# Four narrow full-precision products side by side, and more rooms for what feeds them, in a one-core hybrid decoder step

## The chip, the core and the metric

One core of one Trainium2 chip runs the whole step as one program. The metric is the time of one execution in device microseconds; the kernel before has a median of 2964.94 us over three runs (2961.44 to 2966.86). The engines are named as the profile names them: PE (matrix products), PEld (its weight loads), DVE (vector), ACT (scalar), POOL, and SP, which here only issues DMAs. Each engine runs its own instructions in order.

## What is computed

One layer of a decoder for two groups of tokens that share the weights: a prompt of 2048 tokens, and 32 sample tokens (8 requests of 4 tokens) with states and caches of their own. Cut to what matters:

```python
m, s_gla, s_ssm, conv = mixer(rmsnorm(x, g1), s_gla, s_ssm, conv, lw)   # GLA heads beside Mamba-2 heads; ends in @ w_out
h = x + rmsnorm(m, g2)
q = rmsnorm(h, g3) @ w_xq                                # 4 heads of 256
p = softmax(q @ mem_k.T / 16);  a = (p @ mem_v) @ w_xo   # 256 memory tokens
h = h + rmsnorm(a, g4)
hf = rmsnorm(h, g5)
y = h + rmsnorm((silu(hf @ w_gate) * (hf @ w_up)) @ w_down, g6)         # 2816 features
```

All of it is float32. The outputs are `y` of both groups, the new states, the convolution tails, and the memory keys and values of the prompt.

## The kernel before

**The prompt** comes first in blocks of 512 tokens (function `block`: projections, convolution, both kinds of heads), then in passes of Strassen-like products: `o` (w_out), `s` and `v` (cross-attention, with the weights folded), three passes `g` (gate and up), and four passes `d` (w_down, 2 or 3 of the 11 feature pairs each, 8 units of 256 tokens per pass). A product of two float32 numbers is made of three `fp32r` products (`three`, L125 to L127), for which ACT and DVE split each operand into a larger and a smaller part (L1540/L1542 for the tokens, in tiles `s`; L1609/L1613 for the weights, in tiles `r`). A unit is seven such products in the order `TURN`; each is called an element here. Their sums sit in PSUM banks `accA`, `accB`, `accC`, and ACT (L1920 in the `d` passes) or DVE take them out.

**The weights of a pass** come in pieces (`Pieces`): a piece is loaded into one of three rooms `st` (SP, L1645), split into a room `r`, and the room `st` is loaded again. A pass `d` of three feature pairs has 14 pieces, a pass of two has 7. The pieces of the next pass are made known at the start of the last unit but one (three loads go out), and one piece is split after each element of the last unit; the rest follow in the first unit of the new pass. There are 8 rooms `r`, and a room is taken again only when its old content is used up.

**The 32 sample tokens** have no stage of their own. Their work stands in generators (`samples`, `sample_chunk`, `samples_down`), and each `yield` ends a step. After each element the main loop takes 0.4 steps (in `g`, from the queue `back`) or 0.8 steps (in `d`, from `aux`). Their products are true float32 with only 32 columns of the PE array: the output goes to one of four groups of 32 columns (`tile_position=(0, 32 * g)`), and PE makes two passes over the moving data for each.

- `s_proj` (L1229; w_out, w_xq and w_xo): a step loads 512 KB into one of two rooms `sraw`, and multiplies with two column groups.
- `s_attend` (L1307): scores against the cached keys; a step of four products takes two products in one column group and two in another. The values (L1342): a step of four products, one in each group.
- `samples_down` (L1958): 44 products; a step is one product, with five rooms `w` of 256 KB.
- `sample_mixer`: 8 states of each kind are read twice, each load (`gla_state`, `ssm_state`; L980, L985) going out in the step that uses it, into two rooms.

**In the last pass `d`** each half unit of results lives in one of seven rooms `y`: taken out of PSUM, `yp` (the earlier passes' sum) added by a DMA, normed, `hX` added by a DMA, stored (L1883). For the last two units `yp` and `hX` are read into spare rooms from the start of the last unit but two (L2122, L2123), one of them a room `y`.

**Order.** In the passes the main loop's instructions are pinned to program order on each engine (`pin`); those of the queue `back` in `g`, and the blocks before, are placed by the framework's scheduler. `quad_sums` (L413 to L422) works in block 1 on sums of w_out: two loads, two empty steps, four subtractions on DVE, four stores.

Of the kernel before, what the change touches and what calls it, by code (L numbers as in the profile page):

```python
# [42 lines left out]
def hymba_kernel(ctx: ExitStack, tc: tile.TileContext, a: dict, o: dict, dbg: dict | None = None):  # L43
# [34 lines left out]
    def drain(q):  # L78
        while q:
            step(q)  # L80


    NJ = seq // 256
# [322 lines left out]
    def quad_sums(i, w):  # L406
        pa2 = late["pa2"]
        for u in range(4):
            for c in (slice(0, 256), slice(256, 512)):
                t = []  # L410
                for n in range(2):
                    r = pa2.tile([P, 512], F32, name="fold", bufs=2)
                    nc.gpsimd.dma_start(out=r.rearrange("p (k c) -> p k c", k=2), in_=w[n, u].rearrange("p (k c) -> p k c", k=2)[:, :, c])  # L413
                    t += [r[:, 0:256], r[:, 256:512]]
                r = pa2.tile([P, 2, MEM], F32, name="fraw")
                t += [r[:, 0], r[:, 1]]
                yield
                yield
                for out, x, y in ((4, 2, 0), (5, 3, 4), (2, 3, 2), (1, 1, 5)):
                    nc.vector.tensor_tensor(t[out], t[x], t[y], op=ALU.subtract)  # L420
                for q, at in enumerate((4, 5, 2, 1)):
                    nc.gpsimd.dma_start(out=wX[i, q][:, u, c], in_=t[at])  # L422
                yield
# [506 lines left out]
    def sample_mixer():  # L930
      mixS, rsel, rmk = (sm2[n] for n in ("mixS", "rsel", "rmk"))
      with ExitStack() as mctx:
# [42 lines left out]
        nc.vector.memset(par[64:128, 1:2], 1.0)  # L975


        def gla_state(r):
            t = mt_([P, 2, P], "Gs", bufs=2)
            nc.sync.dma_start(out=t, in_=a["state_gla"][r])  # L980
            return t

        def ssm_state(r):
            t = mt_([P, 512], "Ms", bufs=2)
            nc.sync.dma_start(out=t, in_=a["state_ssm"][r])  # L985
            return t


        yield
# [228 lines left out]


    def s_proj(units, act, out, ss, gain):  # L1220
        for n in range(2):
            ps = mxt()
            for u in range(4):
                w = ps_.tile([P, 1024], F32, name="sraw", bufs=2)
                nc.sync.dma_start(out=w, in_=units[n, u])
                for kk in range(2):
                    kt = 2 * u + kk
                    g0 = (kt % 4) * 32
                    nc.tensor.matmul(ps[g0:g0 + 32], lhsT=act[:, kt], rhs=w[:, kk * 512:(kk + 1) * 512], start=kt < 4, stop=kt >= 4,  # L1229
                                     tile_position=(0, g0))  # L1230
                yield
            sl = slice(n * 512, (n + 1) * 512)
            fold(out[:, sl], ps)
            if ss is not None:
                nc.scalar.activation(ps[:NS], out[:, sl], AF.Square, accum_out=ss[:NS, n:n + 1])
                ga = post_gain(ps_, "ga", gain, n)
                nc.vector.tensor_tensor(out[:, sl], out[:, sl], ga[:NS], op=ALU.mult)

    def s_T(src, gain, scale):
# [46 lines left out]
    def s_attend():  # L1286
# [4 lines left out]

        def load(i):
            if i < 2 * NR:
                t = ps_.tile([P, 4, MEM], F32, name="sraw", bufs=2)
                nc.sync.dma_start(out=t, in_=a["cache_k"][i // 2][:, i % 2 * 4:i % 2 * 4 + 4])
                got.append(t)
        load(0)
        load(1)
        yield
        for r in range(NR):  # L1300
            qm = ps_.tile([P, KT, NS], F32, name="sqm", bufs=1)
            nc.vector.tensor_tensor(qm, q, sm2["rmk"][:, r].rearrange("p s t -> p (s t)").unsqueeze(1).broadcast_to([P, KT, NS]), op=ALU.mult)
            for kt in range(KT):
                hd = kt // 2
                if kt % 4 == 0:
                    kr = got.popleft()
                nc.tensor.matmul(psc[32 * hd:32 * hd + 32, 0:MEM], lhsT=qm[:, kt], rhs=kr[:, kt % 4], start=r == 0 and kt % 2 == 0,  # L1307
                                 stop=r == NR - 1 and kt % 2 == 1, tile_position=(0, 32 * hd))
                if kt % 4 == 3:
                    load(2 * r + kt // 4 + 2)  # L1310
                    yield
        nm = small.tile([P, 8], F32, name="nm")
        sm = small.tile([P, 8], F32, name="sm")
        nc.vector.tensor_reduce(nm[:, 0:1], psc[:, 0:MEM], axis=mybir.AxisListType.X, op=ALU.max, negate=True)
# [12 lines left out]

        def load(i):
            if i < 2 * NR:
                t = ps_.tile([P, D], F32, name="sraw", bufs=2)  # L1330
                nc.sync.dma_start(out=t, in_=a["cache_v"][i // 2][:, i % 2])
                got.append(t)
        load(0)
        load(1)
        yield
        for r in range(NR):
            pm_ = ps_.tile([P, 8, NS], F32, name="sqm", bufs=1)
            nc.vector.tensor_tensor(pm_, pT, sm2["rmk"][:, r].rearrange("p s t -> p (s t)").unsqueeze(1).broadcast_to([P, 8, NS]), op=ALU.mult)
            for mt in range(2):
                vr = got.popleft()  # L1340
                for hd in range(4):
                    nc.tensor.matmul(po[32 * hd:32 * hd + 32, 0:256], lhsT=pm_[:, 4 * mt + hd], rhs=vr[:, hd * 256:(hd + 1) * 256],  # L1342
                                     start=r == 0 and mt == 0, stop=r == NR - 1 and mt == 1, tile_position=(0, 32 * hd))
                load(2 * r + mt + 2)
                yield
        ot = ps_.tile([P, MEM], F32, name="sp_", bufs=1)
        nc.vector.tensor_copy(ot, po[:, 0:256])
# [537 lines left out]
    def after_direct(j, m, y, ss, h, last):  # L1885

        if not last:
            yield
        if last:
            nc.scalar.activation(mxt(), half(y)[0], AF.Square, accum_out=ss[:, 0:1])  # L1890
            nc.vector.tensor_tensor(half(y)[1], half(y)[1], half(gain["ln_ffn_post"])[1], op=ALU.mult)
            rs = rstd_rows(ss)
            nc.vector.tensor_tensor(half(y)[0], half(y)[0], half(gain["ln_ffn_post"])[0], op=ALU.mult)
            for n in (1, 0):
                t = half(y)[n]
                nc.vector.scalar_tensor_tensor(t, t, rs[:, 0:1], half(h)[n], op0=ALU.mult, op1=ALU.add)
# [40 lines left out]
    def samples_down():  # L1937

        m = pd.tile([P, D], F32, name="m")[:NS]
        ss = small.tile([P, 8], F32, name="s_sq", bufs=1)  # L1940
        ws = deque()

        def load(i):
            if i < 2 * FT:
                n, kt = divmod(i, FT)
                w = pd.tile([P, 512], F32, name="w", bufs=5)
                nc.sync.dma_start(out=w, in_=a["w_down"][n, kt // 2, :, (kt % 2) * 512:(kt % 2 + 1) * 512])
                ws.append(w)
        for i in range(4):
            load(i)  # L1950
        yield
        yield
        for n in range(2):
            ps = mxt()
            for kt in range(FT):
                load(n * FT + kt + 4)
                g0 = (kt % 4) * 32
                nc.tensor.matmul(ps[g0:g0 + 32], lhsT=s_f[:, kt].rearrange("p h t -> p (h t)"), rhs=ws.popleft(),  # L1958
                                 start=kt < 4, stop=kt >= FT - 4, tile_position=(0, g0))
# [46 lines left out]
    def enter(k):  # L2006
# [20 lines left out]
        if kind == "d" and i == 0:  # L2027
# [4 lines left out]
            pd.tile([P, 512], F32, name="w", bufs=5)  # L2032
            gain_row(pd, "ln_ffn_post")
            aux.append(samples_down())
            ring[:] = 8, pd
# [60 lines left out]
    for e, (n, i) in enumerate(order):  # L2096
        k, g, left = work[n]
        kind, b, gs = passes[k]
        if i == 0:
# [11 lines left out]
            elif kind == "d":  # L2111
                if n + 3 == len(work):
# [1 line left out]
                    k8 = made[0] % 8  # L2114
                    r = f((ring[1] if k8 == 7 else rp).tile([P, 2 * RW], F32R, name=f"r{k8}"))
                    rooms = [r[:, c * D:(c + 1) * D] for c in range(3)] + [pd.tile([P, D], F32, name="m")]
                    rooms += [stage() for _ in range(3)] + [pd.tile([P, D], F32, name="y", bufs=7)]
                    adds = []
                    for j in (g + 1, g + 2):
                        z, h = [rooms.pop(0), rooms.pop(0)], [rooms.pop(0), rooms.pop(0)]  # L2120
                        for m in range(2):
                            nc.sync.dma_start(out=z[m], in_=yp[j][:, m * D:(m + 1) * D])  # L2122
                            nc.sync.dma_start(out=h[m], in_=hX[rows(j, m)])  # L2123
# [31 lines left out]
            fn()  # L2155
        part(e + ahead_)

        p = coming if work[cur][2] == 1 else now if begins[cur] else None
        if p:
            p.larger()  # L2160
        tick()
# [114 lines left out]
```

## Time and profile before

| What | us or share |
|---|---|
| median of 3 runs | 2964.94 |
| the profiled execution: its time | 2965.97 |
| its span, first to last instruction | 2964.2 |
| PE busy | 2830.4 (95%) |
| DVE busy | 2089.2 (70%) |
| ACT busy | 1526.3 (51%) |
| mean DMA rate | 179 GB/s |
| mean granted PE clock | 0.983 |

How to read the rows that follow in the prediction. A row of the timeline has the start, the length, the engine, the line, what it writes and reads, and how many instructions are merged (`x8`); a bracket tells how long the engine was idle before and what ended that. A row of windows has a stretch of time, its length, the busy time of PE, PEld, DVE, ACT and POOL (with counts of instructions), the granted PE clock, the busy share of the DMA engines, and GB/s. A row of groups has the line, the operation, its tiles, the count, the busy time and the mean length in ns of one. A row of waits has who waited for whom: us in total, times, the longest. A full matmul's row is longer than its share of time, since matmuls are pipelined: time is read from start to start.

### The profile page before, as it was taken

Reading aid. Unit: us, or ns where it says so; the run is one execution under the profiler, and the core shown is the slowest. Engines: PE = TensorE matmul, PEld = TensorE weight load, DVE = VectorE, ACT = ScalarE, POOL = GpSimd, SP = SyncE. Lnnn points to the kernel's source line nnn. Section 1 sums busy time; section 2 is a strip of 40 time slices with the busy share of each in tenths; the row PEclk is TensorE's granted clock in tenths of the full one; section 3 lists DMA queues with packets and bytes.
Section 4 is the critical chain, followed back from the end, with each engine's and each line's share of the span. In section 5 each row is a group of like instructions: output and inputs, shape, how many; then the busy total and the mean of one; then the engine's idle time right before and its main releaser. Section 6 shows DMA issues by size and latency. Waiting matters only on the chain.

```text
span 2964.2 us, 42292 instructions
## 1 busy us (share of the span) xinstructions
PE 2830.4 (95%) x15207; PEld 2385.0 (80%) x15207; DVE 2089.2 (70%) x3915; ACT 1526.3 (51%) x3047; POOL 554.2 (19%) x754
## 2 busy tenths in 40 slices
PE   8999899999988999999899999999999999999996
PEld 8887677787866878888798977889999985587774
DVE  7677676666737787777887867667678884556565
ACT  5545443544446786767655334434455553434453
POOL 2142341221321321035302100001000000011122
PEclk9999999999999999999999999999999999999998
DMA  7345544242256875568745567663243345767797
GB/s 243 121 147 174 174 123 130 80 126 88 79 201 231 295 266 202 189 193 259 257 158 196 173 199 259 221 222 138 95 153 121 126 165 188 234 144 180 169 224 212
DMA packets 154849, 530.02 MB, mean 179 GB/s; under 512 B 19392, under 2 KB 22640, under 8 KB 143120
## 3 DMA queue, kind: packets, MB, share of 16 engines
q1 hardware_dynamic: 93216, 331.81, 34.8%
q0 software_dynamic: 49184, 170.52, 18.7%
q10 hardware_dynamic: 12240, 24.99, 2.6%
q8 instruction: 120, 1.97, 0.3%
q14 instruction: 89, 0.73, 0.1%
HBM read 373.10 MB, written 154.15 MB: 178 GB/s over the span
## 4 chain that ended last, share of the span: by engine, by line
PE 49%; issue 25%; DVE 7%; DMA 5%; ACT 4%; POOL 2%; POOLq 0%; DVEq 0%; ACTq 0%; SPq 0%
PE accA L125 6%; PE accA L126 6%; PE accA L127 6%; PE acc L125 4%; PE acc L126 4%; PE acc L127 4%; PE accC L125 3%; PE accC L127 3%; PE accC L126 3%; PE accB L125 1%; PE mx L1958 1%; PE accB L127 1%; PE accB L126 1%; DVE s L1542 1%; ACT r L1609 1%
## 5 line engine op out<-in xcount | busy, mean ns | idle before, releaser
L125 PE MATMUL accA<-r,s 128*128 128x512 f32 (+2 forms) x1792 | 643.6, 359 | 27.3 <-ACT r L1609 6.8
L127 PE MATMUL accA<-r,s 128*128 128x512 f32 (+2 forms) x1792 | 631.6, 352 | 2.0 <-DVE s L1542 1.9
L126 PE MATMUL accA<-r,s 128*128 128x384 f32 (+2 forms) x1600 | 556.6, 348 | 1.8 <-DVE r L1613 1.8
L125 PEld LDWEIGHTS accA<-r,s 128*128 128x128 f32 x1792 | 340.8, 190 | 103.4 <-issue 24.2
L1540 ACT ACTIVATE s<-sum 128x512 fp32r<-128x512 f32 (+2 forms) x488 | 289.0, 593 | 249.4 <-DVE sum L1522 103.2
L127 PEld LDWEIGHTS accA<-r,s 128*128 128x128 f32 x1792 | 341.0, 190 | 35.2 <-DVE s L1542 3.6
L125 PE MATMUL accC<-r,s 128*128 128x512 f32 (+2 forms) x896 | 322.7, 360 | 27.2 <-ACT y L1920 15.9
L1542 DVE TENSOR_TENSOR s<-sum,s 128x512 fp32r<-128x512 f32 (+2 forms) x488 | 310.6, 644 | 29.6 <-ACT s L1540 23.6
L126 PEld LDWEIGHTS accA<-r,s 128*128 128x128 f32 x1600 | 304.7, 190 | 25.4 <-DVE r L1613 3.9
L127 PE MATMUL accC<-r,s 128*128 128x512 f32 (+2 forms) x896 | 315.8, 352 | 0.2 <-DVE s L1542 0.2
L1542 DVE TENSOR_TENSOR s<-raw,s 128x512 fp32r<-128x512 f32 (+2 forms) x366 | 236.0, 645 | 70.5 <-ACT s L1540 69.2
L126 PE MATMUL accC<-r,s 128*128 128x384 f32 (+2 forms) x800 | 277.9, 347 | 0.3 <-DVE r L1613 0.3
L1540 ACT ACTIVATE s<-raw 128x512 fp32r<-128x512 f32 (+2 forms) x366 | 218.2, 596 | 64.8 <-PE accC L127 59.2
L119 ACT ACTIVATE whi<-wraw 128x1024 fp32r<-128x1024 f32 (+2 forms) x148 | 137.1, 941 | 196.3 <-PE acc L126 99.4
L125 PEld LDWEIGHTS accC<-r,s 128*128 128x128 f32 x896 | 170.4, 190 | 67.7 <-ACT y L1920 22.2
L120 DVE TENSOR_TENSOR wlo<-wraw,whi 128x1024 fp32r<-128x1024 f32 (+2 forms) x148 | 165.1, 1125 | 58.6 <-ACT whi L119 55.8
L127 PEld LDWEIGHTS accC<-r,s 128*128 128x128 f32 x896 | 170.2, 190 | 16.9 <-DVE s L1542 0.9
L125 PE MATMUL acc<-xh,whi 128*128 128x512 f32 (+1 forms) x464 | 168.7, 365 | 8.4 <-ACT xh L280 8.2
L133 POOL TENSOR_TENSOR rs<-ms,nhalf 128x1 f32<-128x1 f32 (+4 forms) x125 | 113.9, 913 | 329.2 <-DVE ms L131 312.9
L127 PE MATMUL acc<-xh,wlo 128*128 128x512 f32 (+1 forms) x464 | 164.9, 357 | 1.7 <-DVE wlo L120 1.7
L126 PE MATMUL acc<-xl,whi 128*128 128x512 f32 (+1 forms) x464 | 164.4, 356 | 0.2 <-DVE xl L281 0.2
L126 PEld LDWEIGHTS accC<-r,s 128*128 128x128 f32 x800 | 152.7, 191 | 10.7 <-DVE r L1613 0.6
(650 smaller groups left out, 5922.2 us busy)
## 6 DMA issues: line engine op xcount, KB each, us to landing
raw<-in_w_gu_dram SPq DMA_DIRECT2D x66, 1024.0 KB, 4.9
wraw<-in_w_in_fm_dram SPq DMA_DIRECT2D x52, 512.0 KB, 3.6
wraw<-in_w_in_tm_dram SPq DMA_DIRECT2D x48, 512.0 KB, 3.7
yp<-y POOLq DMA_DIRECT2D x48, 512.0 KB, 6.8
raw<-aT SPq DMA_DIRECT2D x24, 768.0 KB, 5.1
st<-in_w_down_dram SPq DMA_DIRECT2D x34, 512.0 KB, 6.6
aT<-og POOLq DMA_DIRECT2D x22, 768.0 KB, 4.2
hX<-y POOLq DMA_DIRECT2D x32, 512.0 KB, 6.7
```

What stands on the lines that cost most here:

```text
L119: last[0] = nc.scalar.activation(hi[:, cs], raw[:, cs], AF.Copy)
L120: nc.vector.tensor_tensor(lo[:, cs], raw[:, cs], f(hi)[:, cs], op=ALU.subtract)
L125: nc.tensor.matmul(ps, lhsT=wh, rhs=ah, start=start, stop=False, skip_group_check=more)
L126: nc.tensor.matmul(ps, lhsT=wh, rhs=al, start=False, stop=False, skip_group_check=more)
L127: nc.tensor.matmul(ps, lhsT=wl, rhs=ah, start=False, stop=stop, skip_group_check=more)
L133: nc.gpsimd.tensor_tensor(out=rs[:rows, :cols], in0=ms[:rows, :cols], in1=nhalf[:rows, :cols], op=ALU.pow)
L1540: nc.scalar.activation(h3, v, AF.Copy)
L1542: return lambda: nc.vector.tensor_tensor(l3, v, f(h3), op=ALU.subtract)
L1609: nc.scalar.activation(hi, v, AF.Copy)
L1958: nc.tensor.matmul(ps[g0:g0 + 32], lhsT=s_f[:, kt].rearrange("p h t -> p (h t)"), rhs=ws.popleft(), start=kt < 4, stop=kt >= FT - 4, tile_ ...
```

## The change

- `s_proj`, `s_attend` and `samples_down` issue their products in fours, one for each column group. For the keys, a load takes the even or the odd kt of all heads (four runs of 1 KB in each partition in place of one of 4 KB).
- `sraw` has four rooms in place of two, and the loads go out that much further ahead; `w` has four in place of five, loaded four at a time, five empty steps (`pause(5)`) before their products. `samples_down` so takes 82 steps in place of 56.
- `gla_state` and `ssm_state` load one state ahead, into three rooms.
- `quad_sums`: the first subtraction is not scheduled ahead of the DVE instruction that was last when the step before it began.
- At the end of a `d` pass two pieces of the next pass are split in the last unit but one (after its elements 5 and 4).
- The last half unit's `hX` goes into two rooms `w` in place of a room `y`.

```diff
+    def last_on(engine):
+        for i in reversed(nc.cur_bb.bb.instructions):
+            if i.engine == getattr(mybir.EngineType, engine) and i.name.startswith("I-"):
+                return i.name
+
+    def keep_behind(i, name):
+        tc.add_manual_dep(i.ins, name, ..., reason="order of issue")
...
 # quad_sums
                 yield
+                behind = last_on("DVE")
                 yield
                 for out, x, y in ((4, 2, 0), (5, 3, 4), (2, 3, 2), (1, 1, 5)):
-                    nc.vector.tensor_tensor(t[out], t[x], t[y], op=ALU.subtract)
+                    d = nc.vector.tensor_tensor(t[out], t[x], t[y], op=ALU.subtract)
+                    if behind is not None:
+                        keep_behind(d, behind)
+                        behind = None
...
 # sample_mixer
-        def gla_state(r):
-            t = mt_([P, 2, P], "Gs", bufs=2)
-            nc.sync.dma_start(out=t, in_=a["state_gla"][r])
-            return t
...
+        def ahead_of(name, shape, src):
+            got = deque()
+            def load(r):
+                if r < NR:
+                    t = mt_(shape, name, bufs=3)
+                    nc.sync.dma_start(out=t, in_=src[r])
+                    got.append(t)
+            def state(r):
+                if r == 0:
+                    load(0)
+                load(r + 1)
+                return got.popleft()
+            return state
+        gla_state = ahead_of("Gs", [P, 2, P], a["state_gla"])
+        ssm_state = ahead_of("Ms", [P, 512], a["state_ssm"])
...
 # s_proj (loads four ahead; before: two rooms, each load in the step that uses it)
-            for u in range(4):
-                w = ps_.tile([P, 1024], F32, name="sraw", bufs=2)
-                nc.sync.dma_start(out=w, in_=units[n, u])
-                for kk in range(2):
-                    kt = 2 * u + kk
-                    g0 = (kt % 4) * 32
-                    nc.tensor.matmul(ps[g0:g0 + 32], lhsT=act[:, kt], rhs=w[:, kk * 512:(kk + 1) * 512], start=kt < 4, stop=kt >= 4,
-                                     tile_position=(0, g0))
+            for u in (0, 2):
+                ws = [got.popleft(), got.popleft()]
+                for g in range(4):
+                    nc.tensor.matmul(ps[32 * g:32 * g + 32], lhsT=act[:, 2 * u + g], rhs=ws[g // 2][:, g % 2 * 512:(g % 2 + 1) * 512],
+                                     start=u == 0, stop=u == 2, tile_position=(0, 32 * g))
+                for i in range(2):
+                    load(4 * n + u + 4 + i)
                 yield
...
                 ga = post_gain(ps_, "ga", gain, n)
+                yield
                 nc.vector.tensor_tensor(out[:, sl], out[:, sl], ga[:NS], op=ALU.mult)
...
 # s_attend, keys (sraw bufs=4, here and for the values)
-                nc.sync.dma_start(out=t, in_=a["cache_k"][i // 2][:, i % 2 * 4:i % 2 * 4 + 4])
+                nc.sync.dma_start(out=t, in_=a["cache_k"][i // 2].rearrange("p (h e) m -> p e h m", e=2)[:, i % 2])
...
-            for kt in range(KT):
-                hd = kt // 2
...
+            for e in range(2):
+                kr = got.popleft()
+                for hd in range(4):
+                    nc.tensor.matmul(psc[32 * hd:32 * hd + 32, 0:MEM], lhsT=qm[:, 2 * hd + e], rhs=kr[:, hd], start=r == 0 and e == 0,
+                                     stop=r == NR - 1 and e == 1, tile_position=(0, 32 * hd))
+                load(2 * r + e + 4)
+                yield
...
 # samples_down
-            for kt in range(FT):
-                load(n * FT + kt + 4)
-                g0 = (kt % 4) * 32
-                nc.tensor.matmul(ps[g0:g0 + 32], lhsT=s_f[:, kt].rearrange("p h t -> p (h t)"), rhs=ws.popleft(),
-                                 start=kt < 4, stop=kt >= FT - 4, tile_position=(0, g0))
+            for k0 in range(0, FT, 4):
+                ws = []
+                for kt in range(k0, min(k0 + 4, FT)):
+                    ws.append(pd.tile([P, 512], F32, name="w", bufs=4))
+                    nc.sync.dma_start(out=ws[-1], in_=a["w_down"][n, kt // 2, :, (kt % 2) * 512:(kt % 2 + 1) * 512])
+                yield from pause(5)
+                for g, w in enumerate(ws):
+                    kt = k0 + g
+                    nc.tensor.matmul(ps[32 * g:32 * g + 32], lhsT=s_f[:, kt].rearrange("p h t -> p (h t)"), rhs=w,
+                                     start=kt < 4, stop=kt >= FT - 4, tile_position=(0, 32 * g))
                 yield
...
 # last pass: rooms for the last two units
-                    rooms += [stage() for _ in range(3)] + [pd.tile([P, D], F32, name="y", bufs=7)]
+                    rooms += [stage() for _ in range(3)] + [[pd.tile([P, 512], F32, name="w", bufs=4) for _ in range(2)]]
...
 # main loop
-        p = coming if work[cur][2] == 1 else now if begins[cur] else None
+        p = coming if work[cur][2] == 1 or coming and kind == "d" and work[cur][2] == 2 and i in (5, 4) else now if begins[cur] else None
```

More of the change, by code (lines that the diff above doesn't have):

```diff
@@ L80, in drain @@
             step(q)
+    def last_on(engine):
[3 more added lines that the diff above has]
+    def keep_behind(i, name):
+        tc.add_manual_dep(i.ins, name, mybir.DependencyInfo(mybir.DependencyClass.NoSync, mybir.DependencyReason.DATA), reason="order of issue")
     NJ = seq // 256
@@ L975, in sample_mixer @@
         nc.vector.memset(par[64:128, 1:2], 1.0)
-        def gla_state(r):
-            t = mt_([P, 2, P], "Gs", bufs=2)
-            nc.sync.dma_start(out=t, in_=a["state_gla"][r])
-            return t
[L983 to L986, printed above, removed]
+        def ahead_of(name, shape, src):
[13 more added lines that the diff above has]
+        ssm_state = ahead_of("Ms", [P, 512], a["state_ssm"])
         yield
@@ L1220, in s_proj, with load @@
     def s_proj(units, act, out, ss, gain):
+        got = deque()
+        def load(i):
+            if i < 8:
+                w = ps_.tile([P, 1024], F32, name="sraw", bufs=4)
+                nc.sync.dma_start(out=w, in_=units[i // 4, i % 4])
+                got.append(w)
+        for i in range(4):
+            load(i)
+        yield
+        yield
         for n in range(2):
             ps = mxt()
-            for u in range(4):
-                w = ps_.tile([P, 1024], F32, name="sraw", bufs=2)
-                nc.sync.dma_start(out=w, in_=units[n, u])
-                for kk in range(2):
-                    kt = 2 * u + kk
-                    g0 = (kt % 4) * 32
-                    nc.tensor.matmul(ps[g0:g0 + 32], lhsT=act[:, kt], rhs=w[:, kk * 512:(kk + 1) * 512], start=kt < 4, stop=kt >= 4,
-                                     tile_position=(0, g0))
+            for u in (0, 2):
[5 more added lines that the diff above has]
+                    load(4 * n + u + 4 + i)
                 yield
@@ L1236, in s_proj @@
                 ga = post_gain(ps_, "ga", gain, n)
+                yield
                 nc.vector.tensor_tensor(out[:, sl], out[:, sl], ga[:NS], op=ALU.mult)
@@ L1293, in load @@
             if i < 2 * NR:
-                t = ps_.tile([P, 4, MEM], F32, name="sraw", bufs=2)
-                nc.sync.dma_start(out=t, in_=a["cache_k"][i // 2][:, i % 2 * 4:i % 2 * 4 + 4])
+                t = ps_.tile([P, 4, MEM], F32, name="sraw", bufs=4)
+                nc.sync.dma_start(out=t, in_=a["cache_k"][i // 2].rearrange("p (h e) m -> p e h m", e=2)[:, i % 2])
                 got.append(t)
-        load(0)
-        load(1)
+        for i in range(4):
+            load(i)
         yield
@@ L1302, in s_attend @@
             nc.vector.tensor_tensor(qm, q, sm2["rmk"][:, r].rearrange("p s t -> p (s t)").unsqueeze(1).broadcast_to([P, KT, NS]), op=ALU.mult)
-            for kt in range(KT):
-                hd = kt // 2
[L1305 to L1311, printed above, removed]
+            for e in range(2):
[4 more added lines that the diff above has]
+                load(2 * r + e + 4)
+                yield
         nm = small.tile([P, 8], F32, name="nm")
@@ L1329, in load @@
             if i < 2 * NR:
-                t = ps_.tile([P, D], F32, name="sraw", bufs=2)
+                t = ps_.tile([P, D], F32, name="sraw", bufs=4)
                 nc.sync.dma_start(out=t, in_=a["cache_v"][i // 2][:, i % 2])
                 got.append(t)
-        load(0)
-        load(1)
+        for i in range(4):
+            load(i)
         yield
@@ L1343, in s_attend @@
                                      start=r == 0 and mt == 0, stop=r == NR - 1 and mt == 1, tile_position=(0, 32 * hd))
-                load(2 * r + mt + 2)
+                load(2 * r + mt + 4)
                 yield
@@ L1895, in after_direct @@
                 t = half(y)[n]
-                nc.vector.scalar_tensor_tensor(t, t, rs[:, 0:1], half(h)[n], op0=ALU.mult, op1=ALU.add)
+                nc.vector.scalar_tensor_tensor(t, t, rs[:, 0:1], h[n], op0=ALU.mult, op1=ALU.add)
                 nc.sync.dma_start(out=o["y"][rows(j, m), n * 512:(n + 1) * 512], in_=t)
@@ L1940, in samples_down @@
         ss = small.tile([P, 8], F32, name="s_sq", bufs=1)
[L1941 to L1952, printed above, removed]
         for n in range(2):
             ps = mxt()
-            for kt in range(FT):
-                load(n * FT + kt + 4)
-                g0 = (kt % 4) * 32
-                nc.tensor.matmul(ps[g0:g0 + 32], lhsT=s_f[:, kt].rearrange("p h t -> p (h t)"), rhs=ws.popleft(),
-                                 start=kt < 4, stop=kt >= FT - 4, tile_position=(0, g0))
+            for k0 in range(0, FT, 4):
[8 more added lines that the diff above has]
+                                     start=kt < 4, stop=kt >= FT - 4, tile_position=(0, 32 * g))
                 yield
@@ L2031, in enter @@
             pd.tile([P, 2 * RW], F32R, name="r7")
-            pd.tile([P, 512], F32, name="w", bufs=5)
+            pd.tile([P, 512], F32, name="w", bufs=4)
             gain_row(pd, "ln_ffn_post")
@@ L2122, in hymba_kernel @@
                             nc.sync.dma_start(out=z[m], in_=yp[j][:, m * D:(m + 1) * D])
-                            nc.sync.dma_start(out=h[m], in_=hX[rows(j, m)])
+                            if isinstance(h[m], list):
+                                for c in range(2):
+                                    nc.sync.dma_start(out=h[m][c], in_=hX[rows(j, m), c * 512:(c + 1) * 512])
+                            else:
+                                nc.sync.dma_start(out=h[m], in_=hX[rows(j, m)])
                         adds.append((z, h))
```

## The prediction

> **What bounds the kernel now.** I read the page's summary first, then windows by stage.
>
> ```profile
> span 2964.2 us, 42292 instructions
> PE 2830.4 (95%) x15207; PEld 2385.0 (80%) x15207; DVE 2089.2 (70%) x3915; ACT 1526.3 (51%) x3047; POOL 554.2 (19%) x754
> 1700.00:2000.00 300.00, 295.26 (x1695) 241.99 (x1694) 202.63 (x340) 116.68 (x214) 16.89 (x27) 1.00 0.67 224
> 2440.00:2600.00 160.00, 157.82 (x549) 88.74 (x548) 83.68 (x167) 61.84 (x127) 11.78 (x20) 1.00 0.66 208
> 2680.00:2700.00 20.00, 14.15 (x59) 11.10 (x58) 12.05 (x20) 10.08 (x17) 1.72 (x2) 0.96 0.79 223
> 2800.00:2820.00 20.00, 14.90 (x65) 11.70 (x63) 10.37 (x17) 8.84 (x15) 1.75 (x2) 1.00 0.88 242
> 2880.00:2900.00 20.00, 14.81 (x66) 11.93 (x64) 10.03 (x20) 6.72 (x17) 6.21 (x9) 0.99 1.05 307
> ```
>
> The first two windows hold the sample tokens' work: attention and projections in `g`, `samples_down` in `d`. PE is 98 to 99% busy there, DVE 68 and 52%, ACT 39% in both. So time taken off PE comes off the span, as long as nothing else fills up. The other three are places where PE starves; there a shorter wait counts. All three lie in the `d` passes.
>
> Now what the samples' products cost. The groups give the counts (each product is two rows, one for each pass over the data); the timeline gives the cost, from start to next start.
>
> ```profile
> L1958 PE MATMUL mx<-w,s_f 128*32 128x512 f32 x88 | 46.0, 605 | 1.5 <-DMA w<-in_w_down_dram 1.5
> L1307 PE MATMUL mx<-sraw,sqm 128*32 128x256 f32 x128 | 19.3, 385 | 2.8 <-DMA sraw<-in_cache_k_dram 1.4 <-DVE r L1613 0.8 <-DVE sqm L1302 0.5
> L1229 PE MATMUL mx<-sraw,sT 128*32 128x512 f32 x64 | 16.8, 605 | 0.0
> L1229 PE MATMUL mx<-sraw,mixS 128*32 128x512 f32 x32 | 8.4, 604 | 0.0
> ...
> 2501.30 0.40 PE L126 MATMUL accA<-r,s 128*128 128x512 f32 x1
> 2501.53 0.39 PE L127 MATMUL accA<-r,s 128*128 128x512 f32 x1
> 2501.85 1.04 PE L1958 MATMUL mx<-w,s_f 128*32 128x512 f32 x2
> 2502.82 0.50 PE L125 MATMUL accA<-r,s 128*128 128x512 f32 x1
> 2503.16 0.39 PE L126 MATMUL accA<-r,s 128*128 128x512 f32 x1
> ...
> 1705.68 1.05 PE L1229 MATMUL mx<-sraw,mixS 128*32 128x512 f32 x4
> 1706.66 0.45 PE L127 MATMUL accA<-r,s 128*128 128x384 f32 x1
> ...
> 1792.95 1.06 PE L1307 MATMUL mx<-sraw,sqm 128*32 128x256 f32 x8
> 1793.94 0.44 PE L125 MATMUL accC<-r,s 128*128 128x384 f32 x1
> ...
> 1846.76 0.62 PE L1307 MATMUL mx<-sraw,sqm 128*32 128x256 f32 x2 [0.54 <-DVE sqm L1302]
> 1847.31 0.44 PE L125 MATMUL accA<-r,s 128*128 128x384 f32 x1
> ...
> 1881.86 0.33 PE L125 MATMUL accA<-r,s 128*128 128x384 f32 x1
> 1882.03 0.33 PE L126 MATMUL accA<-r,s 128*128 128x384 f32 x1
> ...
> 1882.47 0.64 PE L1342 MATMUL mx<-sraw,sqm 128*32 128x256 f32 x8
> 1883.04 0.45 PE L125 MATMUL accA<-r,s 128*128 128x384 f32 x1
> ```
>
> One product of 512 columns takes 0.97 us, two in different column groups 0.98. One of 256 takes 0.55, four in four groups (the values) 0.57. The keys' four, two in each of two groups, take 0.99. So groups run at the same time, and only products of one group queue. Around a step PE loses some more in changing over: from L127 at 2501.53 to the second full product at 2503.16 are 1.63 us, where two plain spacings of 0.23 would do. A single costs 1.17, its 0.97 and 0.20. (The full products of the `g` passes, 384 columns, stand 0.17 apart: 1881.86 to 1882.03.)
>
> **The change, part by part.**
>
> *`samples_down`.* 44 singles at 1.17 are 51.5 us. Afterwards ten fours and two pairs; a four I put at a single plus 0.02 (as the values show at 256 columns), 1.19: 14.3. Saved 37.2, all on PE's path.
>
> On PE, in the first `d` pass (`accA` to `accC` are the prompt's products, `w,s_f` the samples'), the row before:
>
> ```order
> L1958 MATMUL mx<-w,s_f 32x512
> L125 MATMUL accA<-r_23712,s 128x512
> L126 MATMUL accA<-r_23712,s 128x512
> L127 MATMUL accA<-r_23712,s 128x512
> L125 MATMUL accA<-r_23712,s 128x512
> L126 MATMUL accA<-r_23712,s 128x512
> L127 MATMUL accA<-r_23712,s 128x512
> L1958 MATMUL mx<-w,s_f 32x512
> ```
>
> The same products now:
>
> ```order
> L1984 MATMUL mx<-w,s_f 32x512 x4
> L134 MATMUL accA<-r_23712,s 128x512
> L135 MATMUL accA<-r_23712,s 128x512
> L136 MATMUL accA<-r_23712,s 128x512
> L134 MATMUL accA<-r_23712,s 128x512
> L135 MATMUL accA<-r_23712,s 128x512
> L136 MATMUL accA<-r_23712,s 128x512
> L134 MATMUL accB<-r_23594,s 128x512
> ```
>
> Four stand together, and the single that followed six full products is gone.
>
> *`s_proj`.* 96 rows, four in a step: 24 pairs at 0.98 + 0.20, 28.3; then 12 fours at 1.20, 14.4. Saved 13.9.
>
> *Keys.* 128 rows, eight in a step: 16 steps, each 0.99 less 0.57: 6.7. The values keep their form.
>
> The trace has no four of 512 columns. The nearest rows bound it by 0.97 (a single) and 1.96 (two pairs in turn); I stay at the low end, since pair and values both say so. The Trainium skill's page "TensorE: Matmul & The Clock Gate", Part 3, has measured four tiles side by side (in rows, 512 columns) at 3.07 times, not 4. A four would then cost 4 x 0.97 / 3.07 = 1.26, an estimate from that page, and the 22 fours 6 us more than in my sum. The rows of this case speak for the smaller price.
>
> *The waits* that the rooms and the order of issue touch: of PE (L699's within block 1, 300 to 430 us), of SP in the `d` passes, of DVE in block 1, and one row of POOL's timeline.
>
> ```profile
> PE mx L1958 <- DMA w<-in_w_down_dram: 1.5, 1, 1.5
> PE mx L1118 <- DVE sBm L1115: 4.8, 1, 4.8
> PE mx L699 <- DVE gt L902: 4.3, 1, 4.3
> SPq L1947 <- PE mx L1958: 39.6, 21, 3.5
> DVE fraw L420 <- DMA fold<-in_w_out_dram: 17.5, 5, 5.2
> 1597.94 1.03 POOL L1120 TENSOR_TENSOR Ms<-Ms,sell 128x512 f32<-128x512 f32 x1 [3.68 <-DMA Ms<-in_state_ssm_dram]
> ```
>
> More rooms for `w` and keys: PE's waits on their loads are 1.5 and 1.4; I take 2.0 (0 to 2.9). SP now waits for a whole four before it reloads `w`, and the prompt's `raw` and `st` loads queue behind it, as they did 21 times before; I cost that at nothing, since PE, which ends that wait, is also what they feed.
>
> States: POOL waited 3.68 for a state, DVE behind POOL, and PE 4.8 for `sBm` behind DVE. A step is 2.5 elements of 12 products at 0.17, 5 us, and a load now goes out one step sooner, more than the 3.68: 4.8 (0 to 4.8). The third room keeps SP from waiting longer than now: the load of state r+1 wants the room of state r-2, as the load of state r did.
>
> `quad_sums`: DVE stood 17.5 us at the head of block 1 for loads; of PE's waits there, 4.3 stands behind DVE. The subtractions now come later, some in block 2, and the scheduler has reordered much around them. Ends: 4.3 gained, 4.3 lost in block 2 by the same mechanism; I take 3.0.
>
> *Two pieces earlier.* A unit of the long passes is 63 products of 0.23, 14.5; of the first pass 42, 9.7. The 14 pieces of the next pass are split during the last unit and the first one after it. At the second boundary (2680) PE lost 5.85 there, so they wanted 2 x 14.5 + 5.85 = 34.9 us. On ACT at the first boundary (`r<-st` are splits), before:
>
> ```order
> L1540 ACTIVATE s<-sum 128x256
> L1920 COPY y<-accA 128x512
> L1540 ACTIVATE s<-sum 128x256
> L1609 ACTIVATE r_24459<-st 128x1024
> L1920 COPY y<-accA 128x512
> ```
>
> and now, five rows around the first split:
>
> ```order
> L1952 COPY y<-accA 128x512
> L1572 ACTIVATE s<-raw 128x256 x2
> L1641 ACTIVATE r_24386<-st 128x1024
> L1990 ACTIVATE mx,s_sq<-m 32x512
> L1572 ACTIVATE s<-sum 128x256
> ```
>
> The first split moved from the last unit's first elements into the unit before. Two elements are 4.1 us in the long passes: gained 4.1 at each of two boundaries, 8.2. But the first boundary was covered by the singles, which stretched its unit to about 16 us (5.6 singles at 1.17 on top of 9.7). Now it has 9.7 + 1.2 + 14.5 + two elements (3) = 28.4 for those 34.9: a new wait of 6.5. Together 1.7 gained (10 lost to 8 gained). Behind a split that waits stand ACT's `y` copies, and PE behind these.
>
> *The last pass.*
>
> ```profile
> 2874.24 0.88 POOL L1883 DMA_DIRECT2D out_y_dram<-y  x1
> 2882.19 0.57 POOL L1883 DMA_DIRECT2D out_y_dram<-y  x1 [2.19 <-DMA y<-hX]
> 2891.16 0.59 ACT L1920 COPY y<-accA 128x512 f32<-128x512 f32 x1 [5.95 <-DMA out_y_dram<-y]
> 2901.99 0.79 PE L125 MATMUL accC<-r,s 128*128 128x512 f32 x1 [7.19 <-ACT y L1920]
> 2922.78 0.47 PE L125 MATMUL accC<-r,s 128*128 128x512 f32 x1 [4.05 <-DVE y L1918]
> ```
>
> ACT waited for the store issued at 2882.19. Without `hX` in a `y` room each copy gets the room freed one store sooner (2874.24), so both of PE's waits, 11.2, could go. The DMA engines are full there (1.05), which hands part back: I take 6.0 (0 to 11.2). On SP, the loads before and now:
>
> ```order
> L2122 DMA st<-yp 128x1024
> L2123 DMA st<-hX 128x1024
> L2122 DMA st<-yp 128x1024
> L2123 DMA y<-hX 128x1024
> L1563 DMA raw<-aT 128x1536
> ```
>
> ```order
> L2148 DMA st<-yp 128x1024
> L2153 DMA st<-hX 128x1024
> L2148 DMA st<-yp 128x1024
> L2151 DMA w<-hX 128x512 x2
> L1595 DMA raw<-aT 128x1536
> ```
>
> Only the last target changed; `w` is idle by then.
>
> *At nothing* I put the new `yield` after the gain's load (ACT issues the load; DVE's product comes a step later), and the larger number of steps of `samples_down`: 82 at 0.8 per element are 103 elements, not quite two of the four `d` passes.
>
> *Sum:* 37.2 + 13.9 + 6.7 + 2.0 + 4.8 + 3.0 + 1.7 + 6.0 = 75.3 from the profiled execution's 2965.97: 2891. That execution lies 1.0 above the median of the runs.
>
> **Rivals.**
>
> *DMA takes over in the first `d` pass.* Its 33 MB (208 GB/s x 160 us) in 123 us are 271 GB/s, share 0.66 x 160 / 123 = 0.86; 307 at 1.05 has been seen, so the mean fits, but not the boundary's peak. If a third of the 37 comes back as waits: 2902.
>
> *Fours cost up to two pairs.* 22 x 0.96 = 21 more: 2911. For it: no row of a four at 512. Against: 0.98 for a pair, 0.57 for the values. The page's 3.07 belongs here and gives 2896.
>
> *The smaller edits give nothing* and the new boundary wait stands: 2965.97 - 57.8 + 6.5 = 2915. For it: waits move on when one goes.
>
> *Slower.* The keys come in runs of 1 KB.
>
> ```profile
> fold<-in_w_out_dram POOLq DMA_DIRECT2D x16, 256.0 KB, 3.8
> ```
>
> With four rooms a load has four steps of 5 us before PE wants it. To lose the 75.3 and 6 more, each of 16 loads must be 5 us later than that, 25 us for 512 KB. This row reads in 1 KB runs: 3.8 for 256 KB, so 7.6. It would end near 2972.
>
> **Chances.** Forecast (2876 to 2904) 0.56; DMA 0.12; fours 0.08; smaller edits 0.16; slower 0.02; better than 2874, with all waits gone at their full size, 0.06. The range 2874 to 2920 leaves out about 0.13. A measurement of this kernel tells 0.2% (6 us) from no change: faster 0.96, same 0.02, slower 0.02.
>
> **What would show it.** L1984 in fours with about 1.0 us to the next full product; PE's busy time down by some 55; keys' steps 0.57; no wait of `y` copies on `out_y_dram`; no wait of L1118's kind on `sBm`; ACT waiting on `st` at the first `d` boundary, with PE idle there by 4 to 9 us and by 1 to 3 at the later two. A four near 2 us, or windows of the first `d` pass with a DMA share near 1 and PE below 90%, would make me wrong.

## The result, and the profile after

The changed kernel takes 2888.15 us (median of 4 runs, 2880.55 to 2891.54), the kernel before 2964.53 in the same comparison. The ratio is 0.9739, 95% interval 0.9718 to 0.9761. Forecast were 2891 and a range of 2874 to 2920. A second comparison of the same program (first experiment) gave 2882.42 and 0.9725 (0.9708 to 0.9743).

The total is as forecast, but three of its terms are not: one was seven times as large, one came out with the other sign, one was about half. They cancelled, so that the total came out this close is in part luck. This section goes by places.

The page's summary of the profiled execution of the changed kernel:

```profile
span 2878.6 us, 42299 instructions
PE 2762.0 (96%) x15207; PEld 2369.9 (82%) x15207; DVE 2083.5 (72%) x3915; ACT 1523.0 (53%) x3045; POOL 556.6 (19%) x754
```

PE's busy time fell by 68.4 us (from 2830.4), its idle time by 17.2 (133.8 to 116.6); together 85.6 of span.

Windows of the places shown of before: the sample tokens' work in `g`, the first `d` pass, the three `d` boundaries, the last pass. Columns: length; busy time of PE, weight load, DVE, ACT and POOL; granted clock; DMA share; GB/s.

```profile
1660.00:1960.00 300.00, 296.56 (x1828) 258.75 (x1827) 225.12 (x386) 128.71 (x240) 22.14 (x36) 1.00 0.70 239
2380.00:2455.00 75.00, 75.00 (x339) 56.57 (x338) 44.84 (x100) 35.06 (x78) 7.17 (x13) 0.97 0.74 235
2460.00:2480.00 20.00, 14.25 (x55) 10.14 (x55) 13.40 (x23) 10.66 (x19) 1.06 (x2) 0.84 0.79 281
2600.00:2620.00 20.00, 15.16 (x60) 11.83 (x59) 13.25 (x21) 11.39 (x19) 1.72 (x2) 0.90 0.77 212
2720.00:2740.00 20.00, 15.07 (x64) 11.85 (x65) 13.92 (x22) 11.98 (x21) 1.75 (x2) 1.00 0.88 238
2820.00:2840.00 20.00, 13.12 (x50) 10.13 (x48) 7.42 (x14) 3.37 (x9) 4.27 (x6) 0.91 1.05 304
```

PE is full in the first `d` pass until its end (75.00 of 75) and starves at all three boundaries and in the last pass. At the later two boundaries and in the last pass it did so before; at the first it did not. The window of the same products there, before and changed:

```profile
2545.80:2588.10 42.30, 42.30 (x154) 25.52 (x154) 30.95 (x52) 23.99 (x42) 2.62 (x5) 1.00 0.82 267
```

```profile
2455.10:2500.10 45.00, 37.27 (x149) 27.45 (x148) 31.86 (x55) 23.65 (x44) 3.87 (x6) 0.89 0.79 255
```

PE is idle there for 7.7 us, and the granted clock is 0.89.

The 12,672 products that `three` issues are the same in both kernels, and all but 14 stand in the same places of PE's order. So the time from one of them to another, from the starts in the timeline, tells where time went:

| stretch (in the changed kernel's time) | before | changed | changed, second profile |
|---|---|---|---|
| block 1, 300 to 460 | 181.85 | 160.16 | 160.14 |
| states, 1555 to 1600 | 50.52 | 45.38 | 45.63 |
| samples in `g`, 1680 to 1990 | 334.94 | 310.11 | 310.13 |
| first `d` pass and its boundary, 2380 to 2577 | 225.36 | 197.00 | 196.72 |
| second boundary, 2577 to 2635 | 54.57 | 58.09 | 55.41 |
| third boundary, 2705 to 2755 | 51.63 | 50.16 | 49.93 |
| last pass, from 2790 | 81.54 | 78.11 | 78.12 |

The price that was disputed, from the timeline (start, duration, operation), with the groups of the four sample steps (busy, mean ns, idle before):

```profile
2414.61 0.39 PE L136 MATMUL accA<-r,s 128*128 128x512 f32 x1
2414.92 1.07 PE L1984 MATMUL mx<-w,s_f 128*32 128x512 f32 x8
2415.92 0.50 PE L134 MATMUL accB<-r,s 128*128 128x512 f32 x1
...
1768.34 0.64 PE L1340 MATMUL mx<-sraw,sqm 128*32 128x256 f32 x8
1768.91 0.45 PE L134 MATMUL accC<-r,s 128*128 128x384 f32 x1
```

```profile
L1984 PE MATMUL mx<-w,s_f 128*32 128x512 f32 x88 | 12.8, 605 | 0.0
L1340 PE MATMUL mx<-sraw,sqm 128*32 128x256 f32 x128 | 10.6, 390 | 0.7 <-DMA sraw<-in_cache_k_dram 0.7
L1260 PE MATMUL mx<-sraw,sT 128*32 128x512 f32 x64 | 8.5, 605 | 0.0
L1260 PE MATMUL mx<-sraw,mixS 128*32 128x512 f32 x32 | 5.3, 604 | 0.0
```

From a four's start (2414.92) to the next full product are 1.00 us; a single took 0.97. The keys' step is 0.57, and the four's group waits for nothing.

The waits that answer to those shown of before: PE's over the whole span, SP's and POOL's (POOL's from 1550 to 1610 us).

```profile
PE accA L134 <- DVE y L1954: 12.0, 5, 5.4
PE accA L134 <- ACT s L1572: 10.3, 3, 6.7
PE accC L134 <- ACT y L1952: 7.9, 5, 3.3
PE accC L134 <- DVE y L1950: 6.0, 2, 3.7
...
PE mx L1140 <- DVE sBm L1137: 2.2, 2, 1.5
```

```profile
SPq L1980 <- PE mx L1984: 37.7, 9, 7.5
SPq L2000 <- DVE m L1232: 11.3, 1, 11.3
POOL Ms L1142 <- DMA Ms<-in_state_ssm_dram: 9.8, 4, 4.1
```

PE waits 2.2 for `sBm` where it was 4.8; POOL still waits for state rows. The waits behind DVE's `y` grew from 4.0 to 12.0, 7.4 of it at the first boundary. New in the last pass is the 6.7 behind ACT's split.

### The profile page after: what moved, and what is told of

Same layout as the page of the kernel before. It is cut to its first block, busy times and chain, and to the rows that moved or that the text cites. A ratio compares the mean times of both kernels' runs of the same rounds, so it can differ in the third digit from the quotient of the medians.

```text
span 2878.6 us, 42299 instructions
## 1 busy us (share of the span) xinstructions
PE 2762.0 (96%) x15207; PEld 2369.9 (82%) x15207; DVE 2083.5 (72%) x3915; ACT 1523.0 (53%) x3045; POOL 556.6 (19%) x754
```

## The experiments

Each was timed against the kernel before, in four to six runs. Times of stretches are between the same products as in the table.

**The change again.** No edit.

> The changed kernel unaltered, for its spread and a second profile. Theory: the profiled execution (span 2878.6) was at the low end of 2880 to 2892, and the same sum of places comes out: block 1 (300 to 480 us) about 21 us shorter than before, a four of 512 columns 1.00 us to the next full product, the first d boundary with a PE wait near 5. Rival: some of these waits come and go between executions, by up to 10 us in one place; then the two profiles differ there.

2882.42 us (2879.14 to 2889.9). Block 1 and the first `d` pass repeat within 0.3 us. The second boundary does not: 55.41 where it was 58.09, and over all profiles below it lies between 52.9 and 60.2. A difference of 3 us there says nothing.

**Without the order in `quad_sums`.**

```
-                behind = last_on("DVE")
...
-                    if behind is not None:
-                        keep_behind(d, behind)
```

> Only the order of issue in quad_sums undone (no subtraction held behind DVE's last instruction). Theory: the 22 us by which block 1 became shorter are this edit's: DVE stands at its head for the fold loads again (17 us in before), PE loses its 330 to 450 us waits again, time about 2909 (2903 to 2912). Rival, the forecast's size: the edit is worth 3, the rest of block 1 came from elsewhere: about 2891.

2909.03 us, ratio 0.9808 (0.9792 to 0.9824), where the unchanged repeat has 0.9725. The stretch of block 1 takes 181.30 again: the forecast's 3 is refuted, and the 22 stands (21.1 by this stretch). The windows of the same products of block 1 in before, the changed kernel and this one:

```profile
301.50:483.40 181.90, 165.49 (x809) 133.41 (x808) 125.14 (x249) 85.87 (x149) 66.95 (x85) 0.95 0.48 150
```

```profile
301.10:461.30 160.20, 157.90 (x809) 128.56 (x808) 114.56 (x232) 82.19 (x146) 52.00 (x59) 1.00 0.45 140
```

```profile
303.90:485.20 181.30, 164.72 (x808) 133.08 (x807) 125.02 (x249) 85.78 (x149) 66.74 (x85) 0.96 0.48 150
```

and this kernel's wait of DVE:

```profile
DVE fraw L429 <- DMA fold<-in_w_out_dram: 14.9, 5, 5.4
```

Without the order DVE stands again for the loads. PE idles 16.4 us over these products in before (181.90 less 165.49) and 2.3 in the changed kernel: 14.1 of the gain. The other 7.6 is busy time (165.49 against 157.90): the same products ran at a granted clock of 0.95, and now at 1.00. Together 21.7.

**Without the two earlier pieces.**

```
-        p = coming if work[cur][2] == 1 or coming and kind == "d" and work[cur][2] == 2 and i in (5, 4) else now ...
+        p = coming if work[cur][2] == 1 else now if begins[cur] else None
```

> Only the two pieces of the next pass that are split a unit earlier undone. Theory: at the d boundaries the weight loads set the pace, not the place of the first splits; the PE loss at the three boundaries stays within 2 us of the changed kernel's 5.4, 7.2 and 5.8, and the time within 4 us of it (2884 to 2892). Rival, the forecast's arithmetic: each later boundary loses 4.1 more and the first one 4.1 more: 12 us slower, 2900.

2887.33 us, 0.974 (0.9725 to 0.9754), within the spread of the changed kernel. By places: the first boundary's stretch (2455 to 2500) takes 47.67 instead of 45.06 and 44.63, the third 51.53 instead of 50.16 and 49.93, the second (56.55) lies between. So the edit is worth about 3 at the first boundary, as the forecast had it, which is more than this expectation's 2, and 1.5 at the third, not 4.1. PE's waits at the first boundary, here and in the second profile of the changed kernel:

```profile
PE accA L134 <- DVE y L1954: 8.9, 3, 4.9
```

```profile
PE accA L134 <- DVE y L1954: 6.7, 2, 4.7
```

**The last features in a `y` room again.**

```
-  ... + [[pd.tile([P, 512], F32, name="w", bufs=4) for _ in range(2)]]
+  ... + [pd.tile([P, D], F32, name="y", bufs=7)]
```

> Only the last features' room undone: they go into one room of y again. Theory: the last 70 us lose what they lost before (a y copy waiting for the store, PE 7.2) but win back the wait for the raw features that stood behind the w rooms' loads (PE 6.7), so the net is small: 2888 to 2893. Rival, the forecast: 6 us slower, 2894.

2887.69 us, 0.974 (0.9724 to 0.9755). The last stretch takes 81.13 instead of 78.11: the edit is worth 3.0. Its waits of PE and ACT in the last 90 us:

```profile
PE accC L134 <- ACT y L1952: 7.3, 1, 7.3
...
ACT y L1952 <- DMA out_y_dram<-y: 12.8, 2, 6.7
```

The old wait of 7.3 is back. In the changed kernel another took its place. Its SP rows and what ended PE's idle time:

```profile
2809.37 4.12 SPq L2151 DMA_DIRECT2D w<-hX  x2
2816.73 0.32 SPq L1595 DMA_DIRECT2D raw<-aT  x1
```

```profile
2830.93 0.77 PE L134 MATMUL accC<-r,s 128*128 128x512 f32 x1 [3.74 <-DVE y L1950]
2843.57 0.79 PE L134 MATMUL accA<-r,s 128*128 128x512 f32 x1 [6.71 <-ACT s L1572]
```

```profile
ACT s L1572 <- DMA raw<-aT: 16.2, 1, 16.2
```

The raw features of the last unit go out behind the loads for the last two units (4 MB): they are issued at 2816.73 and let ACT begin its splits only at 2842.99; PE waits 6.71 for the splits.

**The last features one unit later** (the second half, 2 MB).

```
-                        (loads of both units at the last unit but two)
+                if n + 3 == len(work) or n + 2 == len(work):
+                    j = g + 1
+                    z, h = adds[n + 3 - len(work)]
```

> The last unit's features (yp and hX, 2 MB) are loaded at the start of the last unit but one instead of one unit sooner, so the last raw features no longer stand behind them on SP. Theory: the raw load that came 26 us after its issue lands in time, PE's wait of 6.7 for ACT's split of it goes, nothing takes its place since the last unit starts 30 us later: the last 85 us are 4 to 7 shorter, time 2877 to 2883. Rival: the DMA engines are full there, the features come late and PE waits for the y of the last unit instead: no change, 2883 to 2890.

2879.75 us (2876.45 to 2881.37), 0.971 (0.9694 to 0.9725). The last stretch takes 71.81, 6.3 less. PE's waits from 2790 us on:

```profile
PE accC L134 <- DVE y L1950: 6.4, 2, 4.1
PE accA L136 <- DVE s L1574: 0.9, 1, 0.9
```

The wait for the split is gone, and nothing took its place. SP issues the raw load no sooner than in the changed kernel (26.2 and 26.6 us into the stretch), but 2 MB now stand behind it instead of ahead of it. So it was held by the transfers ahead of it, not by its time of issue.

**The samples' result stored later**, and **both late edits**.

```
         nc.sync.dma_start(out=h, in_=hXs)
-        yield
-        yield
+        yield from pause(5)
         residual([m], ss, NS, [h])
-        yield
+        yield from pause(3)
```

> The sample tokens' last residual waits three steps longer for its load, and its store is issued two steps later. Theory: the store stood 11.3 us at the head of SP's queue at the second d boundary and held back the weights of the next pass; without it that boundary loses about 3 us less (55 from product to product where it took 55.4 to 59.6), time 2880 to 2886. Rival: the boundary is paced by the DMA engines and the rooms, so it stays at 57 and the time at 2882 to 2890.

> late_last and late_ys together. Theory: the two places are 300 us apart and add up; 6 us from the last stretch and 3 to 4 from the second d boundary, a little handed back at the third: 2876 (2873 to 2880). Rival: a queue hold that goes at one boundary comes back at the next (late_ys' third boundary and last stretch were 1 to 2 longer): no better than late_last alone, 2880.

2883.03 us and 2877.83 (0.9721, 0.9705 to 0.9737; 0.9704, 0.9682 to 0.9726). Alone, the second boundary takes 52.93 and the theory looks confirmed; together with the other edit the same boundary takes 58.58. The store's hold of 11.3 us at the head of SP's queue is real and is gone in both, so it is not what makes that boundary long.

**Four steps between loads and products.**

```
-                yield from pause(5)
+                yield from pause(4)
```

> late_last, and samples_down pauses four steps between loads and products instead of five, so it ends some 15 elements sooner, in the middle of the second d pass, away from its boundary. Theory: the store of the samples' result no longer stands before the next pass's weights, the second boundary takes 53 to 54 from product to product as in late_ys and nothing is handed back at the third: 2874 to 2878. Rivals: loads now have a step of 2.6 us less, PE waits for them (2 to 4 per four in the first pass, 2890); or the boundary does not depend on the store and stays at 57, 2880.

2889.54 us, 0.9746 (0.9727 to 0.9764). The store is now in the middle of the second pass, and the second boundary still takes 56.57: the theory falls a second time. The first pass became 16 us longer; the waits for loads that the profile names are 9.9 of it:

```profile
PE mx L1984 <- DMA w<-in_w_down_dram: 9.9, 7, 3.9
```

**One load at each of four steps.**

```
+                    yield
-                yield from pause(5)
+                yield from pause(5 - len(ws))
```

> samples_down loads its four weights one at each of four steps instead of all at once; the products stay four together. Theory: at the first d boundary four loads (1 MB) were issued just ahead of the next pass's pieces, at a DMA share of 1.01 and 387 GB/s; spread out, the PE wait there falls from 5.4 to 2 or 3, time 2880 to 2886. Rival: the boundary wants 34.9 us of splitting where it has 28.4, whatever the loads do: the wait stays 5 or more.

2928.53 us, 0.9878 (0.9861 to 0.9896). Neither: the fourth load had two steps left before its product, and PE waited for it all through the pass.

```profile
PE mx L1985 <- DMA w<-in_w_down_dram: 24.0, 11, 4.4
```

It says nothing on the boundary, but shows what hid the loads' price in the changed kernel: the five steps of pause, with little to spare.

**`samples_down` alone**, in the kernel before.

> The kernel before with samples_down alone changed (fours, loads in fours). Theory, by the forecast's terms: the fours save 37 us (44 x 1.19 to 10 x 1.20 + 2 x 1.18), and the first d boundary, which the singles had covered, loses about 9 us (6.5 and the 3 that the earlier pieces save): 28 us net, 2938. Rival: the boundary's loss comes from the other edits, 37 net: 2929.

2941.74 us (2934.19 to 2951.78), 0.9919 (0.9898 to 0.9939): 24 us. From 2380 to 2577 the gain is 25.7 (225.36 to 199.69), so some 11 are taken back, not 9. The wait itself is near what was expected: over the boundary's products PE is idle for 10.5 us. But the granted clock is 0.89 there, where before had 1.00, and that was not counted. PE's waits from 2440 to 2600:

```profile
PE accA L125 <- DVE y L1922: 8.5, 3, 4.9
PE accA L125 <- ACT y L1920: 1.3, 2, 0.8
```

So the new wait at the first boundary comes with the fours of `samples_down`, and needs no other edit.

**States loaded as before.**

```
-        gla_state = ahead_of("Gs", [P, 2, P], a["state_gla"])
-        ssm_state = ahead_of("Ms", [P, 512], a["state_ssm"])
+        (two rooms, each row loaded in the step that uses it)
```

> The changed kernel with the state rows loaded as before (two rooms, at the step that uses them). Theory: the 5 us that the stretch 1555 to 1600 us became shorter are this edit's: POOL waits for Ms again, PE for sBm 4 to 5 us, time 2889 (2886 to 2893). Rival: the stretch depended on the order of other work there and stays: 2885.

2887.61 us, 0.9738 (0.9719 to 0.9758), no difference that the times can tell. The stretch 1555 to 1600 takes 49.53 instead of 45.4 to 46.6, and PE's wait is back, with a granted clock of 0.93 over the stretch, as in before (1.00 in the changed kernel):

```profile
PE mx L1131 <- DVE sBm L1128: 4.3, 1, 4.3
```

**A fourth staging room for the next pass's weights**, with the late features.

```
+            turn[0] += 1
+            if turn[0] % 4 == 0:
+                return ring[1].tile([P, 1024], F32, name="st4")
...
-        ..., 512, 3, n == 4)
+        ..., 512, 4 if ring[0] == 8 else 3, n == 4)
```

> late_last, and from the second d pass on the next pass's weights have four staging rooms and four loads ahead instead of three (the first d boundary keeps three). Theory: at the second and third boundary the pace is set by the staging rooms, since SP stands 17 to 18 us for DVE to free one and ACT then waits for the load; a fourth room takes the second boundary from 57 to 53 or less and the third from 50 to 47: time 2873 to 2877. Rival: the DMA engines (share 0.97 to 1.03 in the 10 us rows there) set it, more loads in flight only share them: both stay, 2880.

2868.43 us (2864.53 to 2871.14), 0.967 (0.9651 to 0.9689): the fastest kernel here, 11 us under the late features alone. The expectation had one place wrong: the fourth room is open when the second pass's pieces are made, so it serves the first boundary too, and there it does most: 38.82 instead of 44.56. The third takes 46.75 instead of 49.69. The second takes 56.44 instead of 58.41, which is within its spread: the 53 expected there did not come. Waits of PE and of ACT from 2460 to 2500:

```profile
PE accA L134 <- DVE y L1960: 3.7, 2, 2.0
```

```profile
ACT r L1647 <- DMA st<-wT: 4.6, 5, 3.1
```

and the window over that boundary, in the second profile of the changed kernel (45 us) and here (40 us):

```profile
2460.00:2505.00 45.00, 37.92 (x151) 28.13 (x151) 32.55 (x55) 24.27 (x44) 3.87 (x6) 0.89 0.81 266
```

```profile
2460.00:2500.00 40.00, 36.31 (x155) 27.09 (x154) 32.68 (x56) 23.60 (x44) 3.87 (x6) 0.96 0.89 301
```

The DMA engines had room left (0.81); more loads in flight filled it (0.89, 301 GB/s). PE's idle time fell from 7.1 to 3.7 us, and the granted clock rose from 0.89 to 0.96. In before, ACT stood for such loads at the second boundary too (2665 to 2705 us), where the prediction read what the pieces want:

```profile
ACT r L1609 <- DMA st<-in_w_down_dram: 6.3, 2, 5.2
```

## Why the prediction was right, point by point

The whole was right: 2888 and 2882 for 2891. In part that was luck: `quad_sums` gave 18.7 more than its term, and the term of the two pieces some 10 to 13 less. The parts:

- **`samples_down`, 37.2.** Right. A four costs 1.00 and 0.20 for changing over, as taken (1.19). 44 singles at 1.19 less ten fours at 1.20 and two pairs at 1.19 are 37.9. The Trainium skill ("TensorE: Matmul & The Clock Gate", Part 3) measured 3.07 times for four tiles in rows. The four column groups here do better: 4 x 0.97 / 1.00 is 3.9 times. The rival of fours that cost two pairs is out.
- **`s_proj` 13.9 and keys 6.7.** Right: eleven fours and two pairs (the first four was issued in two parts) make 12.9; the keys' steps are 0.57. The whole stretch gave 24.8. Of the rest, some 5, PE's idle time is 1.8 (4.8 to 3.0); what the remainder is stays open. No run undoes these fours alone, but with `samples_down` alone changed the stretch stays long (336.99).
- **Waits on `w` and keys, 2.0.** Right: 1.5 and 1.4 became 0.0 and 0.7. What the prediction did not price is how near the loads now stand: a step of pause less and PE waits 9.9.
- **States, 4.8.** The number is right, at 3 to 5: undone, the stretch takes 3 to 4 us more. The way is not: the wait was to go, but PE's shrank only from 4.8 to 2.2, since POOL still waits for state rows (9.8). That is half of the gain. The other half is busy time, 45.6 to 43.1 us over the stretch, with a granted clock of 0.93 before and 1.00 now. So this hit is luck too.
- **`quad_sums`, 3.0.** The wrong step, by a factor of seven: 21.7. The prediction took the one wait of PE in block 1 that names the held `gt` as what could go, and an equal loss as the other end. But DVE's 17.5 us stood ahead of all its later work, so most of PE's other waits there (`z`, `dA`, `M` and more) had the same cause: 14.1 of 16.4 us went. They also came with a lower clock, which cost 7.6 more. PE's total over block 1 (165.49 of 181.90) and its clock (0.95) held both numbers before the change.
- **Two pieces earlier, 1.7 net.** Wrong in sign; the low end (10 lost) was nearly it. The fours and their waits should save 39.4 from 2380 to 2577, and 28.4 came, so 11 were lost, not 6.5. The first boundary's new wait was found, and its size nearly: PE is idle there for 7.7 and 7.1 us. The step that failed is that a wait was priced at its own length: the clock behind it (0.89, where before had 1.00) makes up about the rest, an estimate: 0.11 of 45 us is 5, a part of it in idle time. The 4.1 each at the later boundaries came to 1.5 at the third and nothing that can be told at the second; PE's idle time there is 5.4 to 7.3 us, where 1 to 3 was the sign. The 34.9 us that the 14 pieces were said to want were read where ACT itself waited for loads (6.3). So they need not be the time of splitting: at the first and third boundary the pace was that of three staging rooms, and with a fourth the same pieces take 5.7 and 2.9 less. At the second, where the 34.9 was read, no run settles it.
- **Last pass, 6.0.** Half: 3.0 to 3.4. The `y` copies' wait on the store went as told (7.2), but what was late next stood in the prediction's own order rows, behind the loads into `w`: the `raw` load. Moving these loads gave 6.3.
- **At nothing:** the longer `samples_down` does end at the second boundary and holds SP for 11.3 us there, which the prediction did not see; the experiments that took it away leave the boundary within its spread.

The DMA rival did not come: in the first pass the share is 0.74 (2380 to 2455) and PE is full, and at its end, where PE starves, the fourth room shows that the engines had room. Why the second boundary varies by 7 us between profiles stays open.

## What to carry to other kernels

Size a stall on an in-order engine by everything queued behind it: compare the fast engine's busy time and granted clock over the whole stretch with what they could be, instead of adding the waits that name the stalled instruction. A need that is read from a place which was itself waiting for loads may be the loads' pace; test it with one more staging room before moving work around it. When a transfer is moved off one wait, read what is queued behind it in the new place: here that was the next loss, and 6 us once moved.

## What was not expected of the hardware

A short PE wait can cost more than itself. After the wait of 3.27 us at the second boundary the timeline of the changed kernel shows full products 0.43 apart instead of 0.23:

```profile
2616.98 0.80 PE L134 MATMUL accC<-r,s 128*128 128x512 f32 x1 [3.27 <-ACT y L1952]
2617.57 0.63 PE L135 MATMUL accC<-r,s 128*128 128x512 f32 x1
2618.00 0.63 PE L136 MATMUL accC<-r,s 128*128 128x512 f32 x1
```

and in the kernel before the window at the head of block 1 has a granted clock of 0.66:

```profile
330.00:340.00 10.00, 5.66 (x19) 4.16 (x18) 7.26 (x16) 2.22 (x3) 5.36 (x11) 0.66 0.61 204
```

If the slow part ran at half clock, that is 6.8 of 10 us, an estimate. In block 1 14.1 us of waiting came with 7.6 us of longer busy time. A shorter wait can be followed by it too, as in the kernel before after one of 1.83 us:

```profile
402.59 1.07 PE L762 MATMUL mx<-xdt,M 128*128 128x64 f32 x8 [1.83 <-DVE M L752]
406.42 0.63 PE L126 MATMUL acc<-wlo,xh 128*128 128x512 f32 x1
406.85 0.63 PE L127 MATMUL acc<-whi,xl 128*128 128x512 f32 x1
407.28 0.63 PE L125 MATMUL acc<-whi,xh 128*128 128x512 f32 x1
```

The Trainium skill ("TensorE: Matmul & The Clock Gate", Part 1) has the clock fall to half after an idle window of about 3.4 us. The spacing of 0.43 fits a clock of half, but a wait of 1.83 us is shorter than that window. Another, of 1.93 us at 379.2, left the clock at 1.00 (380 to 390 us).

Four products of 32 columns, one in each column group, take 2 to 4% more than one: 1.00 against 0.97 to 0.98 us at 512 columns of moving data, 0.57 against 0.55 at 256.
